# Block sums of w_down by accumulating transfers in an encoder layer on one core

## The chip, the core and the metric

The kernel runs on one core of a Trainium2 chip. A core has TensorE (PE; its weight loads are shown as PEld), VectorE (DVE), ScalarE (ACT), GpSimd (POOL) and SyncE (SP), which only issues transfers here, and 16 transfer engines that all queues share. The metric is the device time of one execution in microseconds (us). The time before is the median of three runs, 2455.74 us (2450.14 to 2459.2).

## The reference

One layer of an encoder for 512 tokens of width 2048: a modulated norm, a mixing part (latent attention on one half, a gated recurrence on the other), an output projection, and then an MLP with a squared ReLU. All is float32. The change lies in the second half of the MLP:

```
h = _rmsnorm(x, pre_mlp_g[layer]) * (1.0 + scale_m) + shift_m
y = jnp.square(jax.nn.relu(h @ w_up[layer])) @ w_down[layer]
x = x + gate_m * _rmsnorm(y, post_mlp_g[layer])
```

`w_up` is 2048 x 8192 and `w_down` is 8192 x 2048, both in HBM, each read from there in blocks of 512 KB.

## The kernel before

Every float32 product is made of three TensorE products of reduced precision: each operand is split into a high half H (ScalarE casts it) and a low half L (VectorE subtracts H from the operand), and H·H, L·H and H·L are added in PSUM. `hl` (line 234) does one split: a cast on line 235 and a subtraction on line 236.

The MLP goes over 16 groups of 512 hidden columns. The last group's share of the down product is done plainly in `down_last`. The other 15 are each one **round** of 22 steps: 8 **U** steps make the next group's hidden values (24 matmuls each, `up_mms`), 14 **D** steps make this group's share of the down product (12 matmuls each, `product`). The order of the steps is written out by hand: `FIRST` for the first round, `ROUND` for the next 13, `LAST` for the last.

```
FIRST = "UUUUDDUDDUDDUDDUDDDDDD"
ROUND = "UDUDDUDUDDUDUDDUDUDDDD"
LAST = "UUDUUDUDUDUDUDDDDDDDDD"
```

The 14 D steps are two **sets** of 7, one for each half of the output columns that is worked on (30 sets in all). A set is a 2 x 2 block product done with seven products instead of eight, as in Strassen's method with shared sums: `make_forms` builds seven forms of the hidden values once per round (A11, S1, A12, S4, S3, S2, A22), and `down_weights` builds for each product the operand from the four blocks B11, B12, B21, B22 of w_down. Product f takes form number f, counted from 0. Products 2, 3 and 6 go on adding into the PSUM bank of products 0, 1 and 4; after each product VectorE adds the bank to y or to V (line 1191).

The operands of products 1, 4, 5 and 6 are sums of blocks. VectorE makes them in place, with four subtractions in each set (lines 1139, 1146, 1149, 1152), as B12-B11, B22-B12, then B22 minus the first, then B21 minus that.

What sets the order: `ahead` prepares the weights of a step two steps before its product (`LEAD`), and `down_loads` issues a block's load up to six D steps ahead (`LEAD_LOAD`), on SyncE's queue, into a pool of five block buffers (tag "B", `btile`). Within each engine a scheduler fixes the order of instructions when the kernel is built, and takes for a new block the buffer that is free first. Split weights have few buffers: `split_next` takes the low halves' three in turn (two of "wL", one of "xL"), so the low half for one step is written when the product three steps before has ended. During a few rounds one of the five block buffers holds a partial sum of the modulation (`units`), whose w_mod loads share the queue.

Of the kernel before, what the change touches and what calls it, by code (L numbers as in the profile page):

```python
# [15 lines left out]
ALU = mybir.AluOpType  # L16
# [37 lines left out]
def encoder_layer(ctx: ExitStack, tc: tile.TileContext, a, out):  # L54
    nc = tc.nc
# [894 lines left out]
    with ExitStack() as ph:  # L950
# [6 lines left out]
        for i in range(2):  # L957
            c = 2 * 2048 + 1024 * i
# [60 lines left out]
    with ExitStack() as ph:  # L1019
# [62 lines left out]

        FORMS = ["A11", "S1", "A12", "S4", "S3", "S2", "A22"]

        def form_tiles(f):
# [10 lines left out]
        def make_forms(u):  # L1096
# [4 lines left out]
            def split_form(f, src):  # L1101
                fm[f] = form_tiles(f)
                hl(fm[f][0], fm[f][1], src)

            split_form("A11", A11)
            split_form("A22", A22)
            nc.vector.tensor_tensor(A22, A21, A22, ALU.add)
            split_form("S1", A22)
            split_form("A12", A12)
            nc.vector.tensor_tensor(A21, A11, A21, ALU.subtract)  # L1110
            nc.vector.tensor_tensor(A11, A22, A11, ALU.subtract)
            nc.vector.tensor_tensor(A12, A12, A11, ALU.subtract)
            split_form("S4", A12)
            split_form("S3", A21)
            split_form("S2", A11)
            return fm
# [3 lines left out]

        def down_load(s, b):
            g, c = divmod(s, 2)
            i, j = int(b[1]) - 1, int(b[2]) - 1
            t = btile(b)
            nc.sync.dma_start(t.rearrange("p (k n) -> p k n", k=2),
                              wslice(w_down, 4 * g + 2 * i, 2, 1024 * j + 512 * c, 512))
            raws[s, b] = t

        LOADS = {0: ["B11"], 1: ["B12"], 2: ["B21"], 3: ["B22"]}
        NP = 7 * 2 * (NG - 1)  # L1130

        def down_weights(q):
            s, f = divmod(q, 7)
            B = {b: raws.get((s, b)) for b in ("B11", "B12", "B21", "B22")}
            if f == 0:
                src = B["B11"]
            elif f == 1:
                src = B["B11"]
                nc.vector.tensor_tensor(src, B["B12"], src, ALU.subtract)
            elif f == 2:  # L1140
                src = B["B21"]
            elif f == 3:
                src = B["B22"]
            elif f == 4:
                src = B["B12"]
                nc.vector.tensor_tensor(src, B["B22"], src, ALU.subtract)
            elif f == 5:
                src = B["B11"]
                nc.vector.tensor_tensor(src, B["B22"], src, ALU.subtract)
            else:  # L1150
                src = B["B21"]
                nc.vector.tensor_tensor(src, src, B["B11"], ALU.subtract)
            return split_next(src)

        loaded = [0]

        def down_loads(q):
            while loaded[0] < min(q, NP):
                s, f = divmod(loaded[0], 7)
                for b in LOADS.get(f, []):  # L1160
                    down_load(s, b)
                loaded[0] += 1
# [4 lines left out]
        def product(q, fm, H, L):  # L1167
            s, f = divmod(q, 7)
            g, c = divmod(s, 2)
# [18 lines left out]
            if g == 0 and fresh:  # L1188
                nc.scalar.copy(dst, Xv)
            else:  # L1190
                nc.vector.tensor_tensor(dst, dst, Xv, ALU.add)  # L1191


        def down_last(g, pss):
# [7 lines left out]
            for i in range(8):  # L1202
# [6 lines left out]
                held.append((ap(dH, o, [[512, 2], [1, 512]]), ap(dL, o, [[512, 2], [1, 512]])))  # L1209
            nc.vector.tensor_tensor(y[:, 0:2, 1024:], y[:, 0:2, 1024:], V, ALU.add)  # L1210
            nc.vector.tensor_tensor(y[:, 2:4, :1024], y[:, 2:4, :1024], V, ALU.add)
            nc.vector.tensor_tensor(y[:, 2:4, 1024:], y[:, 2:4, 1024:], V, ALU.add)
            for t in range(NT):
# [99 lines left out]
```

## Time and profile before

| | |
|---|---|
| median of three runs | 2455.74 us |
| the profiled execution | 2451.36 us |
| its span | 2449.6 us |
| busy: TensorE, VectorE, ScalarE, GpSimd | 96%, 73%, 38%, 5% |
| transfers | 341.76 MB, 140 GB/s in the mean |
| granted TensorE clock, mean | 0.991 of full |

The span runs from the first instruction to the last; the profiled execution's own time is 1.8 us longer. A share of busy time is a mean over stages with different limits, so the stage has to be cut out: the down product runs from 1163 us to about 2386 us, the plain last group and the output follow. Waits are given with the engine and line that ended them. Line numbers are those of the kernel before.

### The profile page before, as it was taken

The numbers are of one execution on the slowest core, as the hardware profiler recorded it, in microseconds if no ns is written. First come the engines' busy times: TensorE is split into PE (matmuls) and PEld (weight loads), VectorE is DVE, ScalarE is ACT, GpSimd is POOL, SyncE is SP. The second block draws the span as 40 slices with busy tenths as digits, with TensorE's granted clock in tenths as the row PEclk, the third lists the DMA queues.
The fourth block names the chain that finished last, engine by engine and source line by source line (L and its number), as shares of the span: only waits on it lengthen the run. The fifth ranks groups of instructions, "written<-read, shape, count | busy, mean of one in ns | idle before, by whom it ended". The sixth has DMA issues, their size and how long they took to land.

```text
span 2449.6 us, 29645 instructions
## 1 busy us (share of the span) xinstructions
PE 2348.0 (96%) x11342; PEld 1944.7 (79%) x11342; DVE 1783.2 (73%) x2203; ACT 932.9 (38%) x1423; POOL 119.2 (5%) x127
## 2 busy tenths in 40 slices
PE   4999999999999999979999999999999999999997
PEld 3778888989887777759888788788888888888875
DVE  5984766667867667485688888776777677767777
ACT  5223333333445432374533333333333333333332
POOL 0110211111200000000000000000000000000000
PEclk9999999999999999989999999999999999999998
DMA  9873353535630068455345354333333333333224
GB/s 312 289 242 96 114 170 105 163 112 165 197 86 25 28 209 266 142 202 186 120 140 175 109 192 150 123 110 103 103 104 103 103 104 97 109 96 112 86 69 163
DMA packets 193800, 341.76 MB, mean 140 GB/s; under 512 B 16886, under 2 KB 65148, under 8 KB 192124
## 3 DMA queue, kind: packets, MB, share of 16 engines
q1 hardware_dynamic: 192464, 339.72, 43.8%
q8 instruction: 89, 1.46, 0.3%
q14 instruction: 51, 0.42, 0.1%
q10 hardware_dynamic: 1196, 0.16, 0.0%
HBM read 331.45 MB, written 8.39 MB: 139 GB/s over the span
## 4 chain that ended last, share of the span: by engine, by line
PE 62%; DMA 3%; DVE 3%; ACT 1%; issue 1%; DVEq 0%; ACTq 0%
PE up L232 10%; PE up L230 10%; PE up L231 10%; PE dn L1180 8%; PE dn L1182 8%; PE dn L1181 7%; DMA raw<-in_w_mod_dram 2%; PE wo L231 1%; PE wo L232 1%; PE wo L230 1%; DVE modacc L273 1%; PE pT L899 1%; PE sc L881 1%; PE upl L230 0%; PE upl L231 0%
## 5 line engine op out<-in xcount | busy, mean ns | idle before, releaser
L235 ACT CAST wH<-B 128x1024 fp32r<-128x1024 f32 x210 | 221.1, 1054 | 499.3 <-PE up L231 194.3
L236 DVE TENSOR_TENSOR wL<-B,wH 128x1024 fp32r<-128x1024 f32 x210 | 256.5, 1222 | 185.4 <-issue 69.8
L1180 PE MATMUL dn<-wH,fH 128*128 128x512 f32 x840 | 329.3, 392 | 2.5 <-DVE G L1047 1.8
L1182 PE MATMUL dn<-wH,fL 128*128 128x512 f32 x840 | 327.5, 390 | 0.0
L1181 PE MATMUL dn<-wL,fH 128*128 128x512 f32 x840 | 326.8, 389 | 0.5 <-DVE wL L236 0.5
L216 ACT CAST wH<-raw 128x512 fp32r<-128x512 f32 (+1 forms) x288 | 163.2, 611 | 340.9 <-PE wo L232 59.5
L217 DVE TENSOR_TENSOR wL<-raw,wH 128x512 fp32r<-128x512 f32 (+1 forms) x288 | 199.1, 725 | 88.0 <-issue 44.6
L236 DVE TENSOR_TENSOR wL<-raw,wH 128x1024 fp32r<-128x1024 f32 x136 | 165.9, 1221 | 95.0 <-issue 43.0
L273 DVE SCALAR_TENSOR_TENSOR modacc<-raw,cond,modacc 128x1024 f32<-128x1024 f32 x120 | 158.5, 1321 | 79.5 <-DMA raw<-in_w_mod_dram 79.1
L235 ACT CAST wH<-raw 128x1024 fp32r<-128x1024 f32 x136 | 143.2, 1054 | 187.7 <-PE dn L1182 145.7
L230 PE MATMUL up<-recH,wH 128*128 128x512 f32 (+1 forms) x544 | 207.9, 382 | 0.0
L232 PE MATMUL up<-recH,wL 128*128 128x512 f32 (+1 forms) x544 | 207.8, 382 | 0.0
L231 PE MATMUL up<-recL,wH 128*128 128x512 f32 (+1 forms) x544 | 207.2, 381 | 0.0
L230 PE MATMUL up<-atH,wH 128*128 128x512 f32 (+1 forms) x544 | 206.3, 379 | 0.0
L232 PE MATMUL up<-atH,wL 128*128 128x512 f32 (+1 forms) x544 | 205.9, 379 | 0.0
L231 PE MATMUL up<-atL,wH 128*128 128x512 f32 (+1 forms) x544 | 205.7, 378 | 0.0
L1180 PEld LDWEIGHTS dn<-wH,fH 128*128 128x128 f32 x840 | 157.6, 188 | 37.8 <-DVE G L1047 2.4
L1181 PEld LDWEIGHTS dn<-wL,fH 128*128 128x128 f32 x840 | 157.7, 188 | 34.7 <-DVE wL L236 1.0
L1182 PEld LDWEIGHTS dn<-wH,fL 128*128 128x128 f32 x840 | 157.6, 188 | 34.5
L1191 DVE TENSOR_TENSOR y<-y,dn 128x1024 f32<-128x1024 f32 x142 | 172.2, 1212 | 0.1
L232 PEld LDWEIGHTS up<-recH,wL 128*128 128x128 f32 x544 | 102.0, 187 | 22.3
L231 PEld LDWEIGHTS up<-recL,wH 128*128 128x128 f32 x544 | 102.0, 187 | 21.7
(371 smaller groups left out, 4670.7 us busy)
## 6 DMA issues: line engine op xcount, KB each, us to landing
raw<-in_w_up_dram SPq DMA_DIRECT2D x136, 512.0 KB, 3.8
raw<-in_w_mod_dram SPq DMA_DIRECT2D x128, 512.0 KB, 4.1
B<-in_w_down_dram SPq DMA_DIRECT2D x120, 512.0 KB, 4.2
raw<-in_w_in_dram SPq DMA_DIRECT2D x128, 256.0 KB, 3.2
mraw<-in_w_mod_dram SPq DMA_DIRECT2D x48, 512.0 KB, 5.2
raw<-in_w_out_dram SPq DMA_DIRECT2D x40, 512.0 KB, 4.0
raw<-in_w_in_dram SPq DMA_DIRECT2D x24, 512.0 KB, 5.3
mraw<-in_w_mod_dram SPq DMA_DIRECT2D x32, 256.0 KB, 4.3
```

The lines of the kernel that those rows point to most:

```text
L216: nc.scalar.copy(H[:, o], raw[:, o])
L217: nc.vector.tensor_tensor(L[:, o], raw[:, o], H[:, o].bitcast(F32), ALU.subtract)
L230: nc.tensor.matmul(o, s_h, m_h, start=first, stop=False)
L231: nc.tensor.matmul(o, s_h, m_l, start=False, stop=False)
L232: nc.tensor.matmul(o, s_l, m_h, start=False, stop=last)
L235: nc.scalar.copy(h_out, src)
L236: nc.vector.tensor_tensor(l_out, src, h_out.bitcast(F32), ALU.subtract)
L273: nc.vector.scalar_tensor_tensor(st["acc"][:, :w], v[:, k, :], cond[:, kt:kt + 1], st["acc"][:, :w], ALU.mult, ALU.add)
L1180: nc.tensor.matmul(o, sh, mh, start=first, stop=False, skip_group_check=skip)
L1181: nc.tensor.matmul(o, sh, ml_, start=False, stop=False, skip_group_check=skip)
L1182: nc.tensor.matmul(o, sl, mh, start=False, stop=last, skip_group_check=skip)
L1191: nc.vector.tensor_tensor(dst, dst, Xv, ALU.add)
```

## The change

The sums of w_down's blocks are no longer made by VectorE. Two buffers, X and Y, are filled by a plain load of one block and then added to in place by transfers from GpSimd's queue with `accum_op=ALU.add`. X becomes B12+B11 (for product 1), then has B22 added (product 5) and then B21 (product 6); Y is B22+B12 (product 4). A transfer that only adds can make no differences, so signs are moved: two of the sums that build the forms change sign, one product is subtracted from V, and V is subtracted from two of the blocks of y. Products 4 and 5 change places (`ORDER`), and so do the splits of two forms. The scratch for the descriptors of GpSimd's transfers is doubled. A set now has five plain loads (X, B11, B21, B22, Y) and four accumulating ones.

```diff
+        ORDER = [0, 1, 2, 3, 5, 4, 6]
...
-            nc.vector.tensor_tensor(A22, A21, A22, ALU.add)
+            nc.vector.tensor_tensor(A22, A21, A22, ALU.subtract)
             split_form("S1", A22)
...
-            nc.vector.tensor_tensor(A12, A12, A11, ALU.subtract)
+            nc.vector.tensor_tensor(A12, A12, A11, ALU.add)
             split_form("S4", A12)
+            split_form("S2", A11)
             split_form("S3", A21)
-            split_form("S2", A11)
...
+        def bring(s, name, b):
+            t = raws[s, name] = btile(name)
+            nc.sync.dma_start(t.rearrange("p (k n) -> p k n", k=2), block(s, b))
+
+        def add_to(s, name, b):
+            nc.gpsimd.dma_start(raws[s, name].rearrange("p (k n) -> p k n", k=2), block(s, b), accum_op=ALU.add)
+
+        LOADS = {0: [("X", "B12", "B11"), ("B11", "B11", None)], 1: [("B21", "B21", None)], 2: [("B22", "B22", None)],
+                 3: [("Y", "B22", "B12")]}
+        SOURCE = ["B11", "X", "B21", "B22", "Y", "X", "X"]
...
-            elif f == 1:
-                src = B["B11"]
-                nc.vector.tensor_tensor(src, B["B12"], src, ALU.subtract)
...
+            s, f = q // 7, ORDER[q % 7]
+            hl_ = split_next(raws[s, SOURCE[f]])
+            if f == 1:
+                add_to(s, "X", "B22")
             elif f == 5:
-                src = B["B11"]
-                nc.vector.tensor_tensor(src, B["B22"], src, ALU.subtract)
-            else:
-                src = B["B21"]
-                nc.vector.tensor_tensor(src, src, B["B11"], ALU.subtract)
-            return split_next(src)
+                add_to(s, "X", "B21")
+            return hl_
...
-                for b in LOADS.get(f, []):
-                    down_load(s, b)
+                for name, b, more in LOADS.get(f, []):
+                    bring(s, name, b)
+                    if more:
+                        add_to(s, name, more)
...
-                nc.vector.tensor_tensor(dst, dst, Xv, ALU.add)
+                nc.vector.tensor_tensor(dst, dst, Xv, ALU.subtract if f == 4 else ALU.add)
...
-            nc.vector.tensor_tensor(y[:, 0:2, 1024:], y[:, 0:2, 1024:], V, ALU.add)
+            nc.vector.tensor_tensor(y[:, 0:2, 1024:], y[:, 0:2, 1024:], V, ALU.subtract)
...
-            nc.vector.tensor_tensor(y[:, 2:4, 1024:], y[:, 2:4, 1024:], V, ALU.add)
+            nc.vector.tensor_tensor(y[:, 2:4, 1024:], y[:, 2:4, 1024:], V, ALU.subtract)
...
-    nc = bacc.Bacc("TRN2", target_bir_lowering=False, num_devices=1, dynamic_dma_scratch_size=1024)
+    nc = bacc.Bacc("TRN2", target_bir_lowering=False, num_devices=1, dynamic_dma_scratch_size=2048)
```

GpSimd's queue, which ends before the MLP in the kernel before, now holds 120 transfers. Here are those of three sets from the middle, in the order in which they are issued: X_13314 is the X of the first set of a round, X_13584 that of the second, X_13871 that of the first set of the next round; "x2" are two in a row (B22, then B21).

```order
L1132 DMA X_13584<-in_w_down_dram 128x2x512
L1132 DMA X_13314<-in_w_down_dram 128x2x512 x2
L1132 DMA Y_13706<-in_w_down_dram 128x2x512
L1132 DMA X_13584<-in_w_down_dram 128x2x512
L1132 DMA X_13871<-in_w_down_dram 128x2x512
L1132 DMA X_13584<-in_w_down_dram 128x2x512
L1132 DMA Y_13974<-in_w_down_dram 128x2x512
```

A set's first addition to X is issued ahead of the last additions to the X of the set before.

The second place is VectorE at the end of the last round, from the last sums to the first pieces of the plain last group (`lraw`). Before, with the sums of lines 1149 and 1152 between the splits (`wL<-B`) and the additions of the PSUM banks (`dn`):

```order
L1149 TENSOR_TENSOR B_17513<-B_17662,B_17513 128x1024
L236 TENSOR_TENSOR fL<-u,fH 128x512
L1191 TENSOR_TENSOR y<-y,dn_17770 128x2x512
L236 TENSOR_TENSOR wL<-B_17513,wH 128x1024
L1152 TENSOR_TENSOR B_17612<-B_17612,B_17513 128x1024
L1191 TENSOR_TENSOR y<-y,dn_17825 128x2x512
L236 TENSOR_TENSOR fL<-u,fH 128x512
L236 TENSOR_TENSOR wL<-B_17612,wH 128x1024
L1191 TENSOR_TENSOR V<-V,dn_17839 128x2x512
L236 TENSOR_TENSOR fL<-u,fH 128x512 x2
L236 TENSOR_TENSOR atL<-lraw,atH 128x1024
L1191 TENSOR_TENSOR y<-y,dn_17825 128x2x512
```

And now, from the split of X for product 5 on:

```order
L236 TENSOR_TENSOR wL<-X,wH 128x1024
L236 TENSOR_TENSOR fL<-u,fH 128x512
L1186 TENSOR_TENSOR y<-y,dn_17814 128x2x512
L236 TENSOR_TENSOR wL<-Y,wH 128x1024
L236 TENSOR_TENSOR fL<-u,fH 128x512
L1186 TENSOR_TENSOR y<-y,dn_17832 128x2x512
L236 TENSOR_TENSOR wL<-X,wH 128x1024
L1186 TENSOR_TENSOR V<-V,dn_17885 128x2x512
L236 TENSOR_TENSOR fL<-u,fH 128x512
L236 TENSOR_TENSOR atL<-lraw,atH 128x1024
L1186 TENSOR_TENSOR y<-y,dn_17899 128x2x512
L236 TENSOR_TENSOR atL<-lraw,atH 128x1024 x2
```

The sums are gone from between the splits; the second `wL<-X` stands where the split of B_17612 stood, with the same additions and splits of the last group behind it.

## Rows read from the trace of the kernel before

**Rows 1.** The page, span and busy time of each engine (share of the span, instructions).
```profile
span 2449.6 us, 29645 instructions
PE 2348.0 (96%) x11342; PEld 1944.7 (79%) x11342; DVE 1783.2 (73%) x2203; ACT 932.9 (38%) x1423; POOL 119.2 (5%) x127
```

**Rows 2.** Busy time in four stretches; first column is the stretch in us.
```profile
core 0: us, PE busy (x) PEld busy (x) DVE busy (x) ACT busy (x) POOL busy (x), PEclk, DMA share, GB/s
1163.00:2359.00 1196.00, 1194.22 (x5203) 975.59 (x5202) 895.07 (x844) 431.04 (x484) 0.00 (x0) 1.00 0.38 116
2359.00:2381.00 22.00, 22.00 (x99) 18.14 (x98) 21.17 (x19) 10.56 (x13) 0.00 (x0) 1.00 0.16 48
2381.00:2405.00 24.00, 16.08 (x63) 10.88 (x61) 21.67 (x19) 6.67 (x7) 0.00 (x0) 0.93 0.65 218
```

**Rows 3.** TensorE's waits, 1150 to 2450 us: total us, times, longest us.
```profile
PE upl L230 <- DVE y L1226: 3.6, 1, 3.6
PE upl L231 <- DVE recL L236: 2.2, 2, 1.7
PE dn L1180 <- DVE G L1047: 1.8, 3, 0.9
PE upl L231 <- DVE atL L236: 1.1, 2, 0.7
PE dn L1180 <- ACT wH L235: 0.7, 1, 0.7
PE dn L1181 <- DVE wL L236: 0.5, 1, 0.5
```

**Rows 4.** Timeline of TensorE, two matmuls ten apart: start, length, operation.
```profile
2170.64 0.39 PE L1182 MATMUL dn<-wH,fL 128*128 128x512 f32 x1
...
2172.91 0.39 PE L1180 MATMUL dn<-wH,fH 128*128 128x512 f32 x1
```

**Rows 5.** Instructions on the block buffers, ns min/median/max; one sum line of four.
```profile
L235 ACT CAST wH<-B x210: 1037/1054/1059, 1147.3 to 2381.4; 128x1024 fp32r<-128x1024 f32 x105
L236 DVE TENSOR_TENSOR wL<-B,wH x210: 1211/1224/1227, 1152.3 to 2382.5; 128x1024 fp32r<-128x1024 f32 x105
L1125 SPq DMA_DIRECT2D B<-in_w_down_dram x120: 367/368/1466, 1079.6 to 2352.7; - x120
...
L1146 DVE TENSOR_TENSOR B<-B,B x30: 1212/1223/1228, 1154.8 to 2370.1; 128x1024 f32<-128x1024 f32 x30
...
DMA to landing us min/median/max: 3.6/4.2/10.0
```

**Rows 6.** SyncE's transfer queue: packets, MB, share of 16 engines' span.
```profile
q1 hardware_dynamic: 192464, 339.72, 43.8%
```

**Rows 7.** Busy time with w_mod loads, and without; columns as in rows 2.
```profile
1240.00:1560.00 320.00, 319.18 (x1389) 260.12 (x1388) 264.79 (x247) 112.01 (x125) 0.00 (x0) 1.00 0.49 155
1640.00:2300.00 660.00, 660.00 (x2885) 540.93 (x2884) 483.42 (x457) 235.28 (x265) 0.00 (x0) 1.00 0.34 102
```

**Rows 8.** Timeline of VectorE in the last stage; in brackets idle time before, and releaser.
```profile
2382.46 1.23 DVE L236 TENSOR_TENSOR wL<-B,wH 128x1024 fp32r<-128x1024 f32 x1 [0.77 <-ACT wH L235]
...
2395.52 1.23 DVE L236 TENSOR_TENSOR recL<-lraw,recH 128x1024 fp32r<-128x1024 f32 x1 [1.56 <-ACT recH L235]
...
2404.41 1.88 DVE L1226 TENSOR_TENSOR y<-y,upl 128x512 f32<-128x512 f32 x3
```

**Rows 9.** Timeline of TensorE in the same stage, two of its starts after a wait.
```profile
2382.48 0.50 PE L1180 MATMUL dn<-wH,fH 128*128 128x512 f32 x1 [0.70 <-ACT wH L235]
...
2405.14 0.79 PE L230 MATMUL upl<-atH,fH 128*128 128x512 f32 x1 [3.56 <-DVE y L1226]
```

More of the change, by code (lines that the diff above doesn't have):

```diff
@@ L1111, in make_forms, with block @@
             nc.vector.tensor_tensor(A11, A22, A11, ALU.subtract)
-            nc.vector.tensor_tensor(A12, A12, A11, ALU.subtract)
+            nc.vector.tensor_tensor(A12, A12, A11, ALU.add)
             split_form("S4", A12)
+            split_form("S2", A11)
             split_form("S3", A21)
-            split_form("S2", A11)
             return fm
         raws = {}
-        def down_load(s, b):
+        def block(s, b):
             g, c = divmod(s, 2)
             i, j = int(b[1]) - 1, int(b[2]) - 1
[L1124 to L1127, printed above, removed]
@@ L1129, in encoder_layer @@
-        LOADS = {0: ["B11"], 1: ["B12"], 2: ["B21"], 3: ["B22"]}
+            return wslice(w_down, 4 * g + 2 * i, 2, 1024 * j + 512 * c, 512)
+        def bring(s, name, b):
[5 more added lines that the diff above has]
+                 3: [("Y", "B22", "B12")]}
@@ L1130, in encoder_layer @@
+        SOURCE = ["B11", "X", "B21", "B22", "Y", "X", "X"]
         NP = 7 * 2 * (NG - 1)
         def down_weights(q):
-            s, f = divmod(q, 7)
-            B = {b: raws.get((s, b)) for b in ("B11", "B12", "B21", "B22")}
-            if f == 0:
-                src = B["B11"]
-            elif f == 1:
-                src = B["B11"]
-                nc.vector.tensor_tensor(src, B["B12"], src, ALU.subtract)
-            elif f == 2:
-                src = B["B21"]
[L1142 to L1145, printed above, removed]
-                nc.vector.tensor_tensor(src, B["B22"], src, ALU.subtract)
-            elif f == 5:
-                src = B["B11"]
-                nc.vector.tensor_tensor(src, B["B22"], src, ALU.subtract)
-            else:
-                src = B["B21"]
-                nc.vector.tensor_tensor(src, src, B["B11"], ALU.subtract)
@@ L1167, in product @@
         def product(q, fm, H, L):
-            s, f = divmod(q, 7)
+            s, f = q // 7, ORDER[q % 7]
             g, c = divmod(s, 2)
```

## The prediction

> **What bounds the kernel now.** I read the busy times first, then TensorE's busy time by stage, then who waits for whom on TensorE, and last the end of the program instruction by instruction. The reader is to see that TensorE has almost nothing left to be given. It is busy 96% of the span [rows 1], and the stage that the change touches, from the first w_down product at 1163 us to 2359 us, shows it busy 1194.2 of 1196.0 us [rows 2]. Matmuls follow each other there at a fixed distance: ten of them take 2172.91 - 2170.64 = 2.27 us, so 0.227 us each [rows 4]. A product of 12 matmuls (a D step) therefore takes 2.72 us, a U step of 24 takes 5.44 us, and a round of 8 U and 14 D steps takes 360 x 0.227 = 81.6 us. VectorE is busy 895 of those 1196 us [rows 2]: much used, but not what ends last. All of TensorE's waits after 1150 us come to 9.9 us [rows 3]: 1.8 us behind the gate row G, which the change does not touch, and 8.1 us in the last stage. That stage, 2359 to 2405 us, is different: VectorE is busy 21.2 of 22.0 us, then 21.7 of 24.0, while TensorE falls to 16.1 of 24.0 [rows 2]. So the change can give back at most those 8.1 us, and about 1 us of slower matmuls behind the longest wait, whatever VectorE is spared.
>
> **What is removed.** Four subtractions in each of 30 sets leave VectorE: 120 x 1.22 us = 146 us [rows 5]. In the bulk they lie beside a busy TensorE and are worth nothing. The last set's four, 4 x 1.22 = 4.9 us, lie in the end stage where VectorE is full; they are worth up to that.
>
> **What is added.** Each set now has five plain loads instead of four (30 more SyncE issues of 0.37 us [rows 5], beside a SyncE with time to spare) and four accumulating transfers from GpSimd's queue, 120 in all, of 512 KB each. GpSimd does nothing else in this stage (0.0 busy [rows 2]). The sign changes alter the operation of equal instructions, so their price is nothing; so is that of the order of two products, since each keeps its PSUM buffer's turn. The larger descriptor scratch moves addresses only.
>
> **What decides: the latency T of one accumulating transfer**, from the end of the split that releases the buffer to the landing. X is one buffer that is added to three times. The first sum is ready long ahead. The other two stand in a chain: split for product 1, add B22, split for product 5, add B21, split for product 6. A split is a cast on ScalarE (1.05 us) and a subtraction on VectorE (1.22 us) [rows 5], 2.27 us. How early a split may come is set by its low half: three buffers are used in turn, so VectorE may write the half for step n only when product n-3 has ended.
>
> In a normal round the second set is the tight one, as products 3, 5, 4, 6 are its last four steps (18 to 21). The half for product 5 (step 19) may be written when step 16 ends. From there to the start of product 6 (step 21) lie one U and three D: 5.44 + 3 x 2.72 = 13.6 us. Needed are 1.22 + T + 2.27 us, so nothing waits while T is under **10.1 us**. In the first set three D and two U lie there, 19.0 us: no danger.
>
> In the first round (its last six steps all D) and the last (eight D) the whole chain is tight, from the end of step 13 to the start of step 21. It needs 1.22 + 2T + 2 x 2.27 = 5.8 + 2T. The first round has six D and a U, 21.8 us, and so waits from T = 8.0 on, 2T - 16.0 us. In the last round seven D are 19.0 us: product 6 is late from T = 6.6 on. But there VectorE is what the end hangs on. In the trace the last split of a B block ends at 2383.7 us, and from there VectorE works its way to the first addition of the last product at 2404.4, with 1.56 us idle behind a transfer for the last block of weights [rows 8]; TensorE starts again at 2405.1 [rows 9]. The last set's buffers now come free in the order in which they are used, and no sum reads an older one, so I take that idle time as gone. TensorE would have begun the last product at 2382.48 - 0.70 = 2381.8 us [rows 9], so step 13 ends at 2381.8 - 19.0 = 2362.8, and the last split ends at 2362.8 + 5.8 + 2T = 2368.6 + 2T. Against 2383.7 + 1.56 = 2385.3 the end moves by **2T - 16.7 us**, though by no more than the 8.1 us of waits downward.
>
> **How large is T?** The trace has no accumulating transfer and no transfer from GpSimd. Below it cannot lie under a plain load of the same block, 4.2 us in the median; above, I take the slowest of these 120 loads, 10.0 us [rows 5], with two loads one after the other, 8.4 us, between. An accumulating transfer reads the block and its destination, is set off by software on GpSimd, and meets more traffic than before; I take **8 us**, nearest to the two loads in a row. The traffic: 339.72 MB held the 16 engines 43.8% of 2449.6 us [rows 6], so 512 KB (0.524 MB) holds them 1.66 us. A round had 16 loads, 26.5 us of 81.6, which is the share of 0.34 that the trace shows there [rows 7]. Now it has 18 loads and 8 accumulations; at one or two passes each that is (29.9 + 13.3 to 26.6) / 81.6 = 0.53 to 0.69. In the rounds that also load w_mod, 0.49 before [rows 7], it becomes 0.69 to 0.86: not full, but the landings will be longer there.
>
> One page of the Trainium skill bears on T, Collectives: The Full Stack, section "The bandwidth ceiling: the fold count and why AG ≠ RS ≠ AR". It says that adding in the transfer costs nothing by itself, but that both operands are read on the same queue, and it gives 62.28 against 32.35 GB/s, a factor of 1.93. By it the estimate of T would be 4.2 + 0.93 x 1.66 = 5.7 us, and the sum 2451.4 - 5.3 = 2446.1 us. No run here shows such a transfer yet.
>
> **The sum.** At T = 8: bulk 0, normal rounds 0 (8 is under 10.1), first round 0, end 2 x 8 - 16.7 = -0.7 us. The profiled execution took 2451.36 us for a span of 2449.6, so 2450.7 us in its terms. It is 4.4 us below the median of the three runs, 2455.74; against that median the forecast is **2455.0 us**, no change. As said, about 0.5% (12.3 us) is what a measurement of this kernel can tell from none.
>
> **Waits that the change adds, and who stands behind them.** On ScalarE the cast of X for product 6 waits for the transfer, and the casts of the next weights stand behind it; on VectorE the low half waits, and the additions that empty PSUM stand behind that. On SyncE the load of the next Y waits for X's buffer, and w_up loads stand behind it. All three are idle waits until T passes 10.1 us. On GpSimd's queue, in order, the next set's first addition to X stands ahead of this set's last. Its plain load waits only for the split for product 0 of this set; in the second set that is written when step 10 has ended, and the load lands about 1.2 + 4.2 = 5.4 us later, while the split for product 5 waits for step 16, four D and two U or 21.8 us later. So this costs nothing either.
>
> **Rivals.**
>
> The first is that the change only shows at the end and T is short: one load and one more pass, 4.2 + 1.66 = 5.9 us. Then the end gains 2 x 5.9 - 16.7 = -4.9 us, 2446.5 in the profile's terms and 2451 against the median. The factor of the Trainium skill belongs to the same case.
>
> All of the 8.1 us would still be 0.33%, so even this is "no change". Faster by 12.3 us would need time from where TensorE shows no wait; only a wait that the records hide could give it.
>
> The second is on the other side: **the chain on X becomes the bound.** For it speak the software start, two reads, the doubled traffic, and that nothing in the trace bounds T from above but a slow plain load. Against it speaks the 10.1 us of room in 13 rounds. Its price is (2T - 16.7) + (2T - 16.0) + 13 x (T - 10.1): at 10.4 us it is 4.1 + 4.8 + 3.9 = 12.8 us, which is where it decides. At T = 12 it is 7.3 + 8.0 + 24.7 = 40.0 us, so 2496 us; at 13 it is 57 us, 2513.
>
> The third: the transfer engines fill up in the rounds with w_mod. One accumulation would have to hold them (81.6 - 40.0 - 3.3) / 8 = 4.8 us, nearly three passes, and then w_up comes late too. For about four rounds at a few us each I price it at 10 to 20 us, 2465 to 2475.
>
> The fourth: the change does not do what it says, because GpSimd starts the transfers one behind the other and late. That is a long T by another cause, with the second rival's prices.
>
> **How the numbers follow.** Forecast (T from 6.5 to 10.4): 0.50. Short T with a gain at the end, within 0.5%: 0.10. Hidden gain over 12.3 us: 0.03. Chain on X: 0.28. Full transfer engines: 0.06. Late starts: 0.03. So faster 0.03, within 0.5% 0.60, slower 0.28 + 0.06 + 0.03 = 0.37. Range: below, the floor 2455.7 - 8.1 and some spread of the runs (2450.14 is 5.6 below the median), 2443. Above, it takes in the chain up to T = 12.6, 2505; what is left out is the upper third of the slow cases, about 0.12, and the hidden gain.
>
> **What would show it right or wrong.** Right: TensorE's waits between 1163 and 2359 us stay near 2 us, VectorE loses 146 us, landings from GpSimd's queue have a median under 10 us, and the end moves by a few us. Wrong: TensorE waits in each round for the cast or the low half of X at product 6, first and longest in the last four products of a round, or its matmuls stand further apart. If the landings are over 10.4 us the second rival holds; if they are short and TensorE still waits, I missed a queue.

## The result, and the profile after

The changed kernel takes 2516.3 us (median of 4 runs, 2512.53 to 2519.46) against 2454.22 us for the kernel before (4 runs): a ratio of 1.0256, 95% interval 1.024 to 1.0272. It is slower by 62 us, outside the forecast of 2455.0 us with its range up to 2505. The profiled execution of the changed kernel took 2519.46 us for a span of 2517.7, that is 68.1 us more span than before.

The page of the changed kernel, to be read beside [rows 1] and [rows 6] (span and busy time of each engine; then queues with packets, MB and share of 16 engines):

```profile
span 2517.7 us, 30058 instructions
PE 2371.1 (94%) x11342; PEld 1956.8 (78%) x11342; DVE 1651.2 (66%) x2083; ACT 930.6 (37%) x1423; POOL 266.0 (11%) x247
...
q1 hardware_dynamic: 200624, 355.45, 44.1%
q0 software_dynamic: 32640, 62.92, 15.2%
```

VectorE has lost its 120 subtractions. Their lengths come to 146.4 us, as forecast, and the 2083 that stay grew by 2.0 us together. The busy time of the page falls by only 132.0 us because it counts once the 0.1 us or so by which neighbouring instructions overlap: lengths and busy time differ by 122.2 us before and by 109.8 now. TensorE has the same 11342 matmuls. Its waits after 1150 us have grown from 9.9 us [rows 3] to 52.7 (engine, operation, releaser: total us, times, longest us):

```profile
PE dn L1175 <- DVE y L1186: 39.4, 18, 4.6
PE dn L1175 <- DVE G L1047: 4.7, 3, 3.0
PE upl L230 <- DVE y L1221: 3.3, 1, 3.3
PE upl L231 <- DVE atL L236: 2.4, 2, 2.2
PE dn L1175 <- ACT y L1184: 1.7, 1, 1.7
PE upl L230 <- ACT fH L235: 0.9, 1, 0.9
PE up L230 <- ACT wH L235: 0.3, 1, 0.3
```

The first line is three quarters of it: 18 times, a w_down product waits until VectorE has added an earlier product to y (L1186) and so emptied its PSUM buffer. Before, that line did not exist. The same in the rounds with w_mod and in the plain ones, to be read beside [rows 7] (busy time by stretch, then granted clock, share of the transfer engines, GB/s):

```profile
core 0: us, PE busy (x) PEld busy (x) DVE busy (x) ACT busy (x) POOL busy (x), PEclk, DMA share, GB/s
1243.00:1640.00 397.00, 370.18 (x1545) 297.48 (x1544) 257.37 (x245) 121.56 (x137) 42.36 (x35) 0.96 0.74 192
1640.00:2340.00 700.00, 686.34 (x2980) 558.73 (x2979) 424.37 (x403) 240.80 (x271) 81.40 (x67) 1.00 0.66 163
```

In the plain rounds TensorE loses 13.7 of 700 us, in eight waits of 1.6 to 2.0 us; in the 397 us with w_mod it loses 26.8 us, and the clock is no longer 1.00 throughout. Taken from the starts of all matmuls from the first product to the last: gaps of 0.5 us or more are 36 instead of 8 and 52.4 us longer than the usual distance in sum, and gaps of 0.25 to 0.5 us, most of them 0.43, which is the distance at the low clock, are 112 instead of 12 and cost 16.2 us more. Together 68.6 us, as much as the whole difference of the spans.

**A plain round, read step by step** (timeline, with the idle time before an instruction and its releaser in brackets; some matmuls, loads and casts between are left out):

```profile
1755.30 1.22 DVE L236 TENSOR_TENSOR wL<-X,wH 128x1024 fp32r<-128x1024 f32 x1 [1.30 <-PE dn L1176]
...
1756.93 1.20 POOL L1132 DMA_DIRECT2D X<-in_w_down_dram  x1 [16.97 <-DVE wL L236]
...
1762.89 1.05 ACT L235 CAST wH<-X 128x1024 fp32r<-128x1024 f32 x1 [2.11 <-DMA X<-in_w_down_dram]
...
1763.84 0.59 ACT L1092 ACTIVATE u<-up 128x512 f32<-128x512 f32 x1
...
1764.46 1.22 DVE L1094 TENSOR_TENSOR u<-u 128x1024 f32<-128x1024 f32 x1 [1.82 <-ACT u L1092]
...
1765.61 1.22 DVE L236 TENSOR_TENSOR wL<-X,wH 128x1024 fp32r<-128x1024 f32 x1
...
1766.74 1.21 DVE L1186 TENSOR_TENSOR y<-y,dn 128x1024 f32<-128x1024 f32 x1
...
1768.10 0.47 PE L1175 MATMUL dn<-wH,fH 128*128 128x512 f32 x1 [1.59 <-DVE y L1186]
```

The low half of X for product 5 is done at 1755.30 + 1.22 = 1756.52 us, and GpSimd starts the last accumulation. ScalarE stands 2.11 us at the cast of X for product 6, until the transfer has landed: T = 1762.89 - 1756.52 = 6.4 us, between the prediction's bounds of 4.2 and 10.0. Behind that cast, in ScalarE's queue, stands the fourth relu of the round's hidden activations; behind the relu, on VectorE, the squaring of u, then X's low half, and only then the addition that empties product 3's PSUM buffer. Product 4, which takes that buffer next, is ready to start at 1768.10 - 1.59 = 1766.51 us. So the cast would have had to start 1.59 us earlier: the limit on T is **4.8 us**, not the 10.1 us of the prediction, which looked at product 6 alone. This repeats in every plain round, 9 times from 1640 to 2370 us with 1.6 to 2.0 us each.

**A round with w_mod** (the same chain in round 1; X's low half for product 5, issue, cast, addition, product 4):

```profile
1299.80 1.22 DVE L236 TENSOR_TENSOR wL<-X,wH 128x1024 fp32r<-128x1024 f32 x1
...
1301.42 1.21 POOL L1132 DMA_DIRECT2D X<-in_w_down_dram  x1 [3.39 <-DVE wL L236]
...
1309.93 1.05 ACT L235 CAST wH<-X 128x1024 fp32r<-128x1024 f32 x1 [5.09 <-DMA X<-in_w_down_dram]
...
1313.79 1.21 DVE L1186 TENSOR_TENSOR y<-y,dn 128x1024 f32<-128x1024 f32 x1
...
1315.15 0.76 PE L1175 MATMUL dn<-wH,fH 128*128 128x512 f32 x1 [4.57 <-DVE y L1186]
```

T is 1309.93 - 1301.02 = 8.9 us here, 2.5 us more than in the plain round, and the wait is 3.0 us longer: the wait grows about as T does. GpSimd issues the transfer 0.4 us after the low half in both, so it does not start late; it takes longer. The transfer engines' share in these two stretches fits that (e9 tests it); behind the longer waits comes the low clock:

```profile
1301.00:1310.00 9.00, 9.00 (x41) 7.32 (x40) 4.20 (x5) 2.31 (x5) 1.21 (x1) 1.00 1.04 256
1756.00:1763.00 7.00, 7.00 (x32) 5.65 (x31) 4.71 (x5) 2.94 (x6) 1.20 (x1) 1.00 0.59 128
...
1315.20:1319.00 3.80, 3.80 (x9) 3.03 (x10) 2.67 (x3) 0.08 (x1) 0.00 (x0) 0.50 0.41 141
...
1683.80:1688.00 4.20, 4.20 (x19) 3.49 (x20) 4.09 (x5) 1.16 (x2) 1.13 (x1) 1.00 0.44 132
```

The first two rows are the stretches in which the two X's travel: full engines in round 1 (1.04), 0.59 in the plain round. The last two rows follow a wait of 4.57 us and one of 1.64 us: after the first, 9 matmuls start in 3.8 us at half clock (1.2 GHz), after the second, 19 in 4.2 us at 2.4 GHz. Nor are the second sets alone concerned here, though the prediction saw no danger for the first: three of the seven waits behind additions to y in these rounds (1.8 to 2.1 us) stand in a first set, with X's cast at T = 9.4 to 9.5 us.

### The profile page after: what moved, and what is told of

The parts are those of the page before. It is cut to its first block, busy times and chain, and to the rows that moved or that the text cites. A ratio compares the mean times of both kernels' runs of the same rounds, so it can differ in the third digit from the quotient of the medians.

```text
span 2517.7 us, 30058 instructions
## 1 busy us (share of the span) xinstructions
PE 2371.1 (94%) x11342; PEld 1956.8 (78%) x11342; DVE 1651.2 (66%) x2083; ACT 930.6 (37%) x1423; POOL 266.0 (11%) x247
## 3 DMA queue, kind: packets, MB, share of 16 engines
q0 software_dynamic: 32640, 62.92, 15.2%
## 5 line engine op out<-in xcount | busy, mean ns | idle before, releaser
L1175 PE MATMUL dn<-wH,fH 128*128 128x512 f32 x840 | 338.6, 403 | 45.8 <-DVE y L1186 39.4
L1177 PE MATMUL dn<-wH,fL 128*128 128x512 f32 x840 | 333.3, 397 | 0.0
L1176 PE MATMUL dn<-wL,fH 128*128 128x512 f32 x840 | 332.8, 396 | 0.0
L1132 POOL DMA_DIRECT2D X<-in_w_down_dram x90 | 109.4, 1253 | 1180.1 <-DVE wL L236 595.4
L235 ACT CAST wH<-X 128x1024 fp32r<-128x1024 f32 x90 | 94.6, 1051 | 277.3 <-PE up L231 141.3
L236 DVE TENSOR_TENSOR wL<-B,wH 128x1024 fp32r<-128x1024 f32 x90 | 110.0, 1223 | 121.6 <-issue 80.3
L236 DVE TENSOR_TENSOR wL<-X,wH 128x1024 fp32r<-128x1024 f32 x90 | 110.0, 1222 | 113.0 <-PE dn L1176 40.1
L1186 DVE TENSOR_TENSOR y<-y,dn 128x1024 f32<-128x1024 f32 x142 | 172.2, 1212 | 2.7 <-PE dn L1177 2.7
```

The lines of the kernel that those rows point to most:

```text
L235: nc.scalar.copy(h_out, src)
L236: nc.vector.tensor_tensor(l_out, src, h_out.bitcast(F32), ALU.subtract)
L1175: nc.tensor.matmul(o, sh, mh, start=first, stop=False, skip_group_check=skip)
L1176: nc.tensor.matmul(o, sh, ml_, start=False, stop=False, skip_group_check=skip)
L1177: nc.tensor.matmul(o, sl, mh, start=False, stop=last, skip_group_check=skip)
L1186: nc.vector.tensor_tensor(dst, dst, Xv, ALU.subtract if f == 4 else ALU.add)
```

## The experiments

The first reading of the trace was another one, theory A: that the new order of the products puts product 6 behind product 4 in the same PSUM buffer. Theory B is that a late X holds up in-order queues, theory C that the traffic itself costs. The ratios below are estimated from all runs of both kernels on the same chip and are not quotients of medians; the medians of the kernel before lie between 2450.55 and 2455.97 us there.

| run | median us | ratio to before, 95% interval |
|---|---|---|
| e1: order of products alone | 2456.77 | 1.0005, 0.9996 to 1.0015 |
| e2: no accumulating transfers | 2451.68 | 0.9987, 0.9977 to 0.9997 |
| e3: U step between 4 and 6 | 2489.99 | 1.0138, 1.0123 to 1.0153 |
| e4: old order, with accumulation | 2516.16 | 1.0256, 1.0222 to 1.0291 |
| e5: plain transfers from GpSimd | 2457.39 | 1.0031, 1.0019 to 1.0043 |
| e6: X's last two accumulations unread | 2484.04 | 1.0145, 1.0125 to 1.0165 |
| e7: six block buffers | 2495.87 | 1.0192, 1.017 to 1.0215 |
| e8: U step, six buffers, w_mod spread | 2444.38 | 0.9992, 0.9978 to 1.0006 |
| e9: w_mod spread | 2495.13 | 1.0169, 1.0144 to 1.0194 |
| e10: U step, w_mod spread | 2467.17 | 1.0054, 1.0041 to 1.0067 |
| e11: before, rearranged as e8 | 2447.85 | 0.9977, 0.9967 to 0.9986 |
| e12: e8 once more | 2450.11 | 0.9988, 0.9977 to 0.9999 |
| e13: two pairs exchanged in two queues | 2482.58 | 1.0108, 1.0086 to 1.013 |
| e14: e13, six buffers, w_mod spread | 2460.3 | 1.0031, 1.0019 to 1.0043 |

**e1, the order alone** (in the kernel before; the forms S2 and S3 change places too):

```diff
+        ORDER = [0, 1, 2, 3, 5, 4, 6]
...
-            s, f = divmod(q, 7)
+            s, f = q // 7, ORDER[q % 7]
```

> The kernel before with nothing changed but the order of the products, 0 1 2 3 5 4 6 (and the two last forms made in the order in which they are now used). The sums stay on VectorE, all transfers are those of before. Theory A (the order: product 6 goes on adding in the PSUM buffer that product 4 has just filled, with no product between, so TensorE waits for VectorE's addition to y): a wait of 1.6 to 1.9 us for y L1191 once in each of 15 rounds, 25 us or a little more, and 0 to 17 us of matmuls at the low clock level: 2480 to 2500 us. Theory B (late accumulating transfers hold up the queues of ScalarE and VectorE) and theory C (the added traffic slows everything): no accumulating transfer here, so no change, 2449 to 2460 us.

Theory A falls: no change. The kernel's TensorE waits from 1240 to 2340 us, all of them:

```profile
PE dn L1181 <- DVE G L1047: 1.2, 1, 1.2
PE up L230 <- ACT wH L235: 1.1, 1, 1.1
```

The written order of steps had misled me: in the program 11 matmuls of the next round's first U step stand between products 4 and 6. The product that waits in the changed kernel is 4, for product 3's buffer.

**e2, without the accumulations.**

```diff
-            if f == 1:
-                add_to(s, "X", "B22")
-            elif f == 5:
-                add_to(s, "X", "B21")
...
-                    if more:
-                        add_to(s, name, more)
```

> The changed kernel without its 120 accumulating transfers: X holds B11 and Y holds B12, as loaded, so the sums of the blocks are left out of the computation. The order of the products, the signs and the 150 plain loads stay. Theory A: the wait for y before product 6 stays at 1.6 to 1.9 us in every round, also in rounds 1 to 4 where the changed kernel shows 3.2 to 4.6 us: 2478 to 2500 us. Theory B: nothing waits for an accumulation any more, 2449 to 2458 us. Theory C: the transfer engines' share falls from 0.66 back to 0.36 in the plain rounds and the time goes back with it, 2449 to 2458 us.

Against A again, and for B or C. It also shows the most that the change could give if its transfers cost nothing: 4.3 us.

**e3, more room.** 

```diff
-FIRST = "UUUUDDUDDUDDUDDUDDDDDD"
-ROUND = "UDUDDUDUDDUDUDDUDUDDDD"
-LAST = "UUDUUDUDUDUDUDDDDDDDDD"
+FIRST = "UUUDDUDDUDDUDDUDDDDDUD"
+ROUND = "UUDDDUDUDDUDUDDUDDDDUD"
+LAST = "UUDUUDUDUDUDDUDDDDDDDD"
```

> The changed kernel with all its transfers and its order of products, but in every round's second set (and in the first set of the first and the last round) one U step is moved so that it stands between product 4 and product 6; only the last set of the last round keeps the two back to back. Theory A: the U step, 5.4 us, covers VectorE's addition, the 1.6 to 1.9 us per round vanish and with them most stretches at the low clock; what stays are waits for a late X in rounds 1 to 4, some 5 to 10 us: 2450 to 2475 us. Theory B: X's window from the first accumulation to product 6 grows from 13.6 to 16.3 us; in the plain rounds T of 6.4 us fitted already, so their waits are not this and stay: 2495 us or more. Theory C: the same transfers in the same time, no change: 2505 to 2520 us.

Of the 62 us some 28 are gone: 2490 us lies in no theory's range, 5 us below B's. From 1640 to 2340 us TensorE is busy 700.00 of 700 us, so the plain rounds' wait has vanished, though B had put the change of room at 2.7 us and the wait at product 6. Both theories had missed that the moved U step also moves other work against X's split: in this run's trace ScalarE waits 3.80 us for X at 1752.18 us, and the round's first relu comes only at 1756.91, with nothing urgent behind the cast. In the rounds with w_mod waits of 1.7 to 3.9 us stay.

**e4, the old order of products with the accumulations.**

```diff
-        ORDER = [0, 1, 2, 3, 5, 4, 6]
+        ORDER = [0, 1, 2, 3, 4, 5, 6]
```

> The changed kernel with the old order of products, 0 1 2 3 4 5 6: product 5 stands again between products 4 and 6, but X's last accumulation has only three D steps, 8.2 us, of window in the second set instead of 13.6. Theory A: the wait for y behind product 4 goes; the chain 1.22 + T + 2.27 us at T = 6.4 is 9.9 us, so TensorE now waits 1.7 us a round for the split of X (wL or wH, not y), more in rounds 1 to 4 and in the first and the last: 2480 to 2520 us, with the releaser changed. Theory B: the chain on X was what cost, and it is 5.4 us shorter of room: 13 rounds lose up to 5 us more each, 2550 us or more. Theory C: no change from the changed kernel, 2510 to 2520 us.

The same loss, in the ranges of A and C, though A had fallen in e1. In six of nine plain rounds the releaser is now X's own split (waits of 1.0 to 1.5 us for wH and 0.76 for wL, 1.7 to 2.2 us together); in three of them an addition to y is again ahead of it, 2.7 to 2.8 us. B's 5 us a round did not come. What A took over from the prediction, the chain on X, gives 9.9 - 8.2 = 1.7 us here, and that is about what these six rounds show: with so little room the prediction's chain does bind. In the changed kernel the room is 13.6 us, and the chain cannot be what costs.

**e5, the same transfers without adding.**

```diff
-            nc.gpsimd.dma_start(raws[s, name].rearrange("p (k n) -> p k n", k=2), block(s, b), accum_op=ALU.add)
+            nc.gpsimd.dma_start(raws[s, name].rearrange("p (k n) -> p k n", k=2), block(s, b))
```

> The changed kernel whose 120 transfers from GpSimd overwrite instead of adding: same queue, same order, same waits, but the sums are left out of the computation. Theory B, as the runs so far narrow it (X for product 6 lands after T; its cast and its low half stand in the queues of ScalarE and VectorE ahead of the addition that empties product 3's PSUM buffer, so product 4 waits by T - 4.8 us, from 6.4 us and a wait of 1.6 us in a plain round and 8.9 us and 4.6 us in a w_mod round): a plain transfer from this queue should have T of 5.2 to 5.8 us, so the wait falls to 0.4 to 1.0 us in a plain round: 2465 to 2495 us. Theory C (traffic, whoever waits for it): a plain transfer moves fewer passes, the share falls from 0.66 to about 0.5 and the time falls to 2455 to 2470 us without waits behind the additions to y.

2457 us is below B's range and inside C's, so the time alone speaks for C. But T is shorter than B had assumed: 4.5 to 4.9 us in the plain rounds, at the limit of 4.8, and one wait of 0.3 us is left from 1640 to 2340 us. Between B and C this run cannot decide; e6 and e13 do. The queue and the landing (last row: median us of the 90 transfers to X), where the changed kernel has 15.2% and 6.6:

```profile
q0 software_dynamic: 17280, 62.92, 8.1%
...
X<-in_w_down_dram POOLq DMA_DIRECT2D x90, 512.0 KB, 4.8
```

Adding therefore costs 15.2% of 2517.7 us / 120 = 3.19 us of the 16 engines for 512 KB, against 8.1% of 2456.1 / 120 = 1.66 us for the plain transfer.

**e6, the traffic with nobody waiting for X's chain.**

```diff
-        SOURCE = ["B11", "X", "B21", "B22", "Y", "X", "X"]
+        SOURCE = ["B11", "X", "B21", "B22", "Y", "B22", "Y"]
```

> The changed kernel with all 120 accumulating transfers, paced as before by X's first split, but products 5 and 6 take their weights from B22 and Y, so that no split waits for X's second and third accumulation; these products get the wrong blocks. The traffic is that of the changed kernel. Theory B: no wait behind the additions to y in the plain rounds, little in rounds 1 to 4: 2449 to 2465 us, with the transfer engines' share still 0.6 or more. Theory C: the traffic is what costs, 2500 to 2520 us.

Neither B nor C: the result lies between. By stretch:

```profile
1243.00:1640.00 397.00, 374.69 (x1584) 300.72 (x1583) 256.73 (x245) 125.74 (x140) 42.82 (x36) 0.98 0.74 196
1640.00:2340.00 700.00, 700.00 (x3056) 572.42 (x3055) 441.54 (x423) 252.26 (x286) 80.91 (x67) 1.00 0.66 166
```

In the plain rounds the traffic costs nothing, at a share of 0.66. With w_mod 22.3 us of 397 are lost with no split waiting for X's last two additions: VectorE's own queue stands for rows of w_mod there (idle before, releaser), and the addition to y behind them:

```profile
1294.54 1.28 DVE L273 SCALAR_TENSOR_TENSOR modacc<-raw,cond,modacc 128x1024 f32<-128x1024 f32 x1 [6.12 <-DMA raw<-in_w_mod_dram]
```

So there are two causes: X's place in the queues in every round, and crowded rounds 1 to 4. One thing is not separated here: e6 also keeps the buffers of B22 and Y longer, which may add to the crowding.

**e7, a sixth block buffer.** The sums of w_mod live in one of the five.

```diff
-NB = 5
+NB = 6
...
-    nc = bacc.Bacc("TRN2", target_bir_lowering=False, num_devices=1, dynamic_dma_scratch_size=2048)
+    nc = bacc.Bacc("TRN2", target_bir_lowering=False, num_devices=1, dynamic_dma_scratch_size=1024)
```

> The changed kernel with six block buffers instead of five (and the descriptor scratch at its old size to make the room). Theory D (in rounds 1 to 4 the row of w_mod sums holds one of the five buffers, so that X and Y are loaded late): the waits of 3.2 to 4.6 us there fall to the 1.6 to 2.0 us of the plain rounds, and the low clock behind them goes: 2485 to 2505 us. Theory B: what decides there is T, 8.9 us beside transfer engines busy 0.75 to 0.84, and a buffer more does not shorten it: 2508 to 2520 us, the plain rounds as they were.

For theory D in the sum, 17 us less loss against the kernel before on the same chip. But it was not the even relief expected: from 1240 to 1640 us two waits of 4.6 and 5.2 us stay, while the others are 1.6 to 2.5 us (15.7 us in sum instead of 26.8). In those two X takes 7.1 and 6.7 us; it is the low half for product 5 that is late, behind a row of w_mod for which VectorE stood 2.80 and 5.40 us. A late transfer holds up a queue there too.

**e8, everything together:** e3's steps, e7's buffers, and w_mod's units behind every second U step.

```diff
-                    if g > 0:
+                    if g > 0 and i % 4 == 0:
                         interleave(units, 1)
```

> The changed kernel with the moved U step, six block buffers, and w_mod's 34 units spread over twice as many rounds (one behind every second U step). Theory B: T in these rounds comes nearer to the 6.4 us of the plain ones, and the moved U step gives room for that: at most a wait of 1 us in each of eight rounds, and the end stage gives back some us: 2450 to 2466 us, as good as before. If T stays at 8 to 9 us wherever w_mod is loaded, eight rounds instead of four wait 2 to 4 us: 2490 to 2520 us.

The median is 6 us below the range, the ratio 0.9992: all of the loss is gone, with every accumulating transfer still there.

**e9 and e10, its parts.** e9 is the changed kernel with the spread units alone, e10 has e3's steps as well.

> The changed kernel with one difference: w_mod's 34 units are spread over twice as many rounds. Two causes are now told apart: in the plain rounds X's accumulation lands 1.6 us later than the queue of VectorE allows; in rounds 1 to 4 the transfer engines are full for some us at a time (share 1.04 from 1301 to 1310 us), so that X and the rows of w_mod land late and VectorE's queue stands. If the second is right, the waits of 3.2 to 4.6 us fall to some 1.6 to 2.5 us and their low clock goes, while every round keeps its wait of 1.6 us: 15 x 1.7 = 26 us, 2475 to 2490 us. If the rounds with w_mod were slow for another reason (the order of GpSimd's queue, five block buffers), eight rounds are slow instead of four: 2510 to 2540 us.

> The moved U step and the spread w_mod together, with five block buffers as in the kernel before. If the two causes are X's room and the full transfer engines, the sixth buffer is not needed: 2443 to 2460 us. If the buffer that the row of w_mod sums holds was the cause, its rounds wait 2 to 4 us each, eight of them: 2465 to 2490 us.

e9 misses its range, 2495 us, but shows what it was for: the waits behind additions to y from 1300 to 1940 us, the rounds that now load w_mod, are 1.5 to 1.9 us, as in a plain round, and none is longer. T in these rounds' second sets is 6.2 to 6.6 us, where in rounds 1 to 4 of the changed kernel it is 8.0 to 8.9. One of five buffers holds w_mod's sums here too, so that alone does not make X late: it takes the loads of w_mod in close order. e10, 2467 us, lies at the lower end of its second case: the crowding is also one of buffers. With five of them TensorE waits 4.8 us once for the G row, a wait that e8, with six, does not have; but eight rounds with 2 to 4 us each, as that case had it, are not in the trace.

**e11 and e12, what the change is worth when nothing waits for it.** e11 is the kernel before with the steps, buffers and units of e8; e12 is e8 again.

> The kernel before, sums on VectorE and old order of products, with the moved U step, six block buffers and spread w_mod. It tells what the rearrangement alone does, without accumulating transfers. Expected: no change, 2447 to 2457 us, since TensorE waits only 1.8 us in these rounds before; then whatever the next kernel gains beside it comes from the 120 subtractions taken from VectorE in the end stage, at most some 5 us.

> The changed kernel with the moved U step, six block buffers and spread w_mod, once more, beside the kernel before with the same rearrangement, so that the two differ only by the change itself. If the change is worth its end stage, it is 2 to 6 us faster than that one; if the traffic takes it back, the two are the same within 2 us. Against the kernel before: 2443 to 2453 us.

The ratio of the two is 0.9988 / 0.9977 = 1.0011, with overlapping intervals: the change gives nothing, not even in the end stage. The rearrangement alone takes 6.5 us from the kernel before, less than the 0.5% that a measurement is sure of. TensorE's waits, first e12, then e11 (1150 to 2500 us):

```profile
PE dn L1175 <- ACT wH L235: 3.6, 1, 3.6
PE upl L230 <- DVE y L1221: 2.2, 1, 2.2
PE dn L1175 <- DVE y L1186: 0.6, 1, 0.6
```

```profile
PE upl L230 <- DVE y L1226: 4.5, 1, 4.5
PE dn L1180 <- DVE V L1191: 0.6, 2, 0.4
```

In these two traces what VectorE saves at the end (2.2 instead of 4.5 us) X's chain in the last round takes back: the 3.6 us are for the cast of Y, which stands in ScalarE's queue behind a cast of X whose transfer took 8.6 us.

**e13, the queue order alone.** The relus are written where the last U step ends, so that X's split can be tied behind them; tied are two pairs, in every second set but the first round's:

```diff
...
+            if behind:
+                with tc.issue_after(last_["relu"].ins):
+                    nc.scalar.copy(H, src)
+                with tc.issue_after(last_["y3"].ins):
+                    nc.vector.tensor_tensor(L, src, H.bitcast(F32), ALU.subtract)
...
```

> The changed kernel, same transfers, same buffers, same order of products on TensorE, with two pairs exchanged in two queues in every round but the first: on ScalarE the cast of X for the second set's product 6 now stands behind the round's fourth relu instead of ahead of it, on VectorE the low half of X for product 6 stands behind the addition of product 3 to y instead of ahead of it. If the wait of a plain round is that order (late X holds up work that TensorE needs earlier than X itself), the nine waits of 1.6 to 2.0 us after 1640 us vanish at unchanged landings, and part of those in rounds 1 to 4 with their low clock: 2460 to 2490 us. If product 6's own weights are late (the chain on X as the prediction had it, T over 10.1 us), the waits stay as large and their releaser becomes wH or wL of X at product 6: 2505 us or more.

As B said. In the two traces the order of all instructions on TensorE and of all transfers from GpSimd is the same; ScalarE and VectorE differ from the changed kernel by 13 exchanged pairs each, one a round from the second to the last but one (in the last the order was so already). The same place in a plain round:

```profile
1737.58 1.20 POOL L1140 DMA_DIRECT2D X<-in_w_down_dram  x1 [16.85 <-DVE wL L236]
...
1741.71 0.60 ACT L1100 ACTIVATE u<-up 128x512 f32<-128x512 f32 x1 [0.29 <-PE up L232]
...
1743.60 1.06 ACT L1068 CAST wH<-X 128x1024 fp32r<-128x1024 f32 x1 [1.28 <-DMA X<-in_w_down_dram]
...
1744.47 1.22 DVE L1194 TENSOR_TENSOR y<-y,dn 128x1024 f32<-128x1024 f32 x1
...
1745.61 1.22 DVE L1070 TENSOR_TENSOR wL<-X,wH 128x1024 fp32r<-128x1024 f32 x1
```

X lands no sooner: 6.0 us from issue to cast, as in the changed kernel (1762.89 - 1756.93). But the relu no longer stands behind the cast, nor the addition to y behind the low half, and TensorE is busy 699.89 of the 700 us from 1640 on. With 33 us of the loss gone, this is a little over half of it.

**e14** adds e7's buffers and e8's spread units to e13.

> The same exchange in the two queues, with w_mod spread over twice as many rounds and six block buffers, and the U steps left where the changed kernel has them. If the loss of the changed kernel is the order in the queues plus the crowded rounds with w_mod, nothing is left of it: 2443 to 2458 us. If the moved U step of the earlier kernels did more than give X room, some 10 to 20 us stay: 2465 to 2480 us.

A miss by 2 us of the range: 7 us of the 62 stay. Of these, one wait of 6.0 us is in the first round, which e13 leaves as it was (there ScalarE empties the buffers).

## Why the prediction was wrong

**The step that failed** is "All three are idle waits until T passes 10.1 us", under the waits that the change adds. The prediction named who stands behind a waiting cast or low half, among them "the additions that empty PSUM", but gave them the deadline of the waiting instruction's own result, product 6. In an in-order queue the deadline is that of the most urgent instruction behind. Here that was product 3's addition, needed by product 4, the product ahead of 6, and on the way to it stood the relu on ScalarE and the squaring of u. That moves the limit by one product, 2.7 us, and by the longer chain, 5.2 us from the cast to product 4 (1768.10 - 1762.89) instead of 2.3 to product 6: 10.1 - 2.7 - 2.9 = 4.5 us, and 4.8 by the trace, where the low half for product 5 came 0.3 us sooner than the prediction had it. e13 shows it by exchanging these two pairs and nothing else. What was needed stood in the program before it ran: each engine's order is fixed when the kernel is built, and it has X's cast ahead of the fourth relu and X's low half ahead of the addition. The prediction's last sign, short landings and TensorE still waiting, is what came; what it had missed was not a queue, though, but the deadline of what stands in one that it had named.

**T itself** was sized well: 6.4 us in plain rounds, 8.9 us in a round with w_mod, within its bounds of 4.2 and 10.0, though 6.4 is just under the 6.5 from which the forecast's own case counted. With T as measured the second rival, the chain on X, costs nothing in the normal rounds: no T there reaches 10.1. It had the right resource; that its price at T = 13 (57 us) is near the 62 measured is chance.

**The traffic** was sized well too: forecast 0.53 to 0.69 in plain rounds, 0.69 to 0.86 with w_mod; measured 0.66 and 0.74. The landings were longer there, as it said; "not full" failed, since the mean of a round hides stretches at 1.04. The third rival, with its 10 to 20 us for four rounds, was real (spreading w_mod took 21 us off). It came beside the waits of every round, not instead of them, and without its condition: an accumulation held the engines 3.19 us, not 4.8. The prediction also left out the waits for the gate row as untouched by the change; they grew from 1.8 to 4.7 us.

**The removed sums** were worth nothing in the bulk, as said, and the end moved little, as said: waits of the last stage come to 8.4 us against 8.1 before (forecast at T = 8: -0.7 us). At the T of 6.7 to 6.8 us measured there the same sum would have given some 3 us back, and the waits show none of it. e2's 4.3 us agree with the first rival's size, for transfers that cost nothing.

**The order of two products** at no price was right (e1). I doubted it wrongly after seeing the result.

**The first round** was to wait from T = 8.0 on; it waits 1.7 us at a lower T, by the same failed step, with ScalarE emptying the buffers.

**The clock** had no term for waits that the change adds. Some 16 of the 68 us are matmuls at the low level, most of them behind the longer waits.

The Trainium skill's page Collectives: The Full Stack, section "The bandwidth ceiling: the fold count and why AG ≠ RS ≠ AR", compares two collectives, and puts the factor of 1.93 between them down to an addition that reads both operands on one queue; the factor in the traces here agrees, 3.19 / 1.66 = 1.92, though no row shows which reads go where. The T drawn from that page of the Trainium skill, an estimate of 5.7 us, was a little short of the 6.4 measured, and the sum drawn from it, 2446.1 us, failed by the same deadline.

**What stays open:** how much of the crowded rounds is the transfer engines and how much the fifth buffer. Either remedy alone takes 17 to 21 us (e7, e9), and they overlap: on top of e13's order both together take 22 us (e14).

## What to carry to other kernels

When a change makes an instruction wait, look in its queue for the most urgent instruction behind it, follow that to the next engine, and set the limit by that one; the waiting instruction's own consumer may have twice the time. Moving work from VectorE to the transfer engines bought nothing here, where VectorE was not what ended last, and it cost most where the engines' share was near 1 for some us, which a mean over a round does not show. If such a transfer must be waited for, put the wait behind what others need first: here that gave back half the loss with no transfer made faster.

## What was not expected of the hardware

- An accumulating transfer of 512 KB held the 16 engines for 3.19 us against 1.66 us plain on the same queue, in 32640 instead of 17280 packets for the same 62.92 MB, and GpSimd spent 1.21 us on issuing it instead of 0.72 us (medians of 120).
- Waits differ in what follows them. In the changed kernel's w_down rounds after the first the granted clock stayed at 1.00 after waits of 1.56 to 1.88 us; after 1.99, 2.09, 3.02, 3.17, 4.01, 4.34 and 4.57 us it was 0.54, 0.53, 0.50, 0.56, 0.59, 0.50 and 0.50 in the next 3.4 to 3.8 us, so a long wait cost more than its length. The length alone does not decide: in the last stage of the same trace, 1.00 followed a wait of 2.17 us, and in e4 a wait of 2.77 us.
- With X's last two additions unread, the same transfers cost TensorE nothing at a share of 0.66 over 700 us (e6).
